# One gathered row at a time, paired score blocks and a partly rounded value product in a Hymba/PEER encoder layer

## The chip, the cores and the metric

One core of one Trainium2 chip runs the whole layer as one program. The metric is the device time of one execution, in microseconds (us).

## The reference

Two sequences of 256 tokens, each with 16 meta tokens ahead, go through one encoder layer of width 1024: norm, one input projection, a short gated convolution beside attention, an output projection, and then a retrieval mixer (PEER). The mixer is what the change is about. Each token scores 16 sets of 128 keys, picks 16 experts of 16384 for each of 8 heads, and mixes them:

```python
def chunk(args):
    xc, ic, gc = args
    uc = jnp.take(u_tab, ic, axis=0)
    a = jax.nn.gelu(jnp.einsum('thkd,td->thk', uc, xc), approximate=False) * gc
    vc = jnp.take(v_tab, ic, axis=0)
    return jnp.einsum('thk,thkd->td', a, vc)
```

So a token takes 128 rows of `u_tab` (a dot with its x, then gelu, then the gate) and the 128 rows of `v_tab` with the same numbers (a weighted sum). All inputs are float32.

## The kernel before, in words

The kernel does the mixer in two ways at once. The **second sequence** is done densely: all 16384 experts are multiplied with its 256 tokens. The **first sequence** is done sparsely: 2 tiles of 128 tokens times 128 picks are 256 gathered rows, one row a partition, each DMA bringing u and v beside each other (8 KB a partition, 1.0486 MB in all). The stages, in order:

1. `front(0, ...)` and `projections`: the first sequence's layer and its keys, with weights split in two rounded parts (`whi`, `wlo`) and three products for one; it gives the picks of tile 0.
2. `front(1, ...)` and `projections` for the second sequence (190 to 401 us in the profile). Beside it run tile 1's picks and the first gathered rows.
3. The scores (401 to 907 us): 128 blocks of 128 experts. A 512 KB load of `u` on SP's queue, 8 matmuls into one PSUM bank `pSj`, gelu on ACT, into the big tile `A` (`Al`, `Ah`). The task `gates_dense` runs beside it: it builds the dense gates by one-hot products on TensorE (`oi`, `gh`, `gl` into `pgm`), four tokens at a time, and multiplies them into `A`.
4. The values (907 us to the end): 128 blocks, each a 512 KB load of `v` and four 512-column matmuls in full float32, A(j) times v, that accumulate in four PSUM banks `acc`.

Rows are gathered through stages 2 to 4. `bg(us)` is called after each piece of TensorE work with an estimate of its length; a share of it (`SF` in the front, `SR`, `SS`, `SMAX` later) is credited, and each 2.65 us of credit calls `gather()`. In stage 4 the calls are spread evenly over the blocks, by `left`. One call of `gather()` takes, for a ring of four row buffers: the gelu and gate of the row whose dot is done (`g_weight`, two one-column ops on ACT), the dot of the oldest row that is on its way (`g_dot`, on DVE), the value sum of the row before (`g_val`, on DVE, into `h`), and then the DMA of a new row into the freed buffer (`g_issue`, on POOL's queue, tied by `sync_dep` to the latest matmul). When tile 0's last row is summed, `h` is stored and the next `h` is loaded into the same buffer, and so is the next `x`.

A scheduler places the instructions of each engine; the code fixes only what it names in a dependency. DVE, ACT and POOL each work strictly in their order, so whatever stands behind a waiting instruction waits too.

Names: `grow` is a gathered row, `dots` its dots, `xg` and `hg` the tile's x and h (after the change both `xh`), `w` a weight slab, `tau` how many tokens' gates are done, `r_done` how many score blocks are in `A`. In the profile, L63 is the line of the helper through which DVE and ACT instructions are recorded.

## Time and profile before

| | |
|---|---|
| median of 3 runs | 1365.17 us (1362.3 to 1374.88) |
| the profiled execution's own time | 1362.99 us |
| its span | 1360.9 us |
| busy: TensorE, DVE, ACT, POOL | 1298.1, 1031.9, 437.4, 414.0 us |
| DMA moved | 460.19 MB, mean 338 GB/s |
| busy time of the 256 dots and 256 value sums on DVE | 312.5 and 327.9 us |
| DVE idle ahead of dots, ended by a row's DMA | 138.6 us |
| DVE idle ahead of value sums, ended by ACT | 67.9 us |

The span is what the profile covers; the execution took 2.1 us more. Busy times of different engines overlap. A wait is the idle time of an engine before an instruction, put down to what ended it; idle time of an engine on which nobody waits costs nothing.

### The profile page before, as it was taken

How to read it: one execution, taken by the hardware profiler on the slowest of the kernel's cores; microseconds unless marked ns; L12 is line 12 of the kernel's file. 1: busy time of each engine (PE TensorE's matmuls, PEld its weight loads, DVE VectorE, ACT ScalarE, POOL GpSimd, SP SyncE). 2: the span in 40 equal slices, each digit the busy share in tenths (PEclk: the TensorE clock that was granted, in tenths of full speed). 3: DMA queues.
4: the chain of work that ended last, by engine and by line, in shares of the span. 5: the costliest groups of instructions: out<-in, count | busy, mean ns of one | idle time of the engine just before them, and what ended most of it. 6: DMA issues, size and time to landing. Idle time of an engine off the chain costs nothing. (4 is left out here: it accounts for less than half of the span.)

```text
span 1360.9 us, 17663 instructions
## 1 busy us (share of the span) xinstructions
PE 1298.1 (95%) x5870; PEld 927.9 (68%) x5870; DVE 1031.9 (76%) x2356; ACT 437.4 (32%) x1467; POOL 414.0 (30%) x480
## 2 busy tenths in 40 slices
PE   5999998998999887999999999999999999999998
PEld 5888986677888666888888888774443344444443
DVE  5656999776999889988888996676666665666665
ACT  4555533732221312555555543111111111111111
POOL 2111224331344342222221221223455523433331
PEclk9999999999999998999999999999999999999999
DMA  6434637577998999999999999999999999999997
GB/s 218 126 109 153 206 107 263 199 272 301 366 341 332 390 399 374 348 368 367 355 368 359 366 375 376 377 416 416 417 417 417 418 416 417 416 417 416 416 417 294
DMA packets 90234, 460.19 MB, mean 338 GB/s; under 512 B 10512, under 2 KB 11024, under 8 KB 57120
## 3 DMA queue, kind: packets, MB, share of 16 engines
q0 software_dynamic: 37296, 270.02, 49.7%
q1 hardware_dynamic: 50832, 182.33, 36.1%
q10 hardware_dynamic: 2016, 6.72, 1.3%
q8 instruction: 46, 0.75, 0.2%
q14 instruction: 44, 0.36, 0.1%
HBM read 454.81 MB, written 4.19 MB: 337 GB/s over the span
## 5 line engine op out<-in xcount | busy, mean ns | idle before, releaser
L157 POOL DMA_INDIRECT grow<-in_uv,eidx x256 | 331.9, 1297 | 694.8 <-PE acc L947 118.1
L130 PE MATMUL pSj<-xr,u 128*128 128x256 f32 x2048 | 465.6, 385 | 12.6 <-ACT Al L63 10.5
L130 PEld LDWEIGHTS pSj<-xr,u 128*128 128x128 f32 x2048 | 386.3, 192 | 68.7 <-ACT Al L63 14.5
L63 DVE SCALAR_TENSOR_TENSOR grow<-grow,xg 128x1024 f32<-128x1024 f32 x256 | 312.5, 1221 | 143.6 <-DMA grow<-in_uv,eidx 138.6
L63 DVE SCALAR_TENSOR_TENSOR hg<-grow,dots,hg 128x1024 f32<-128x1024 f32 x256 | 327.9, 1281 | 77.4 <-ACT dots L63 67.9
L947 PE MATMUL acc<-v,Al 128*128 128x512 f32 x752 | 329.9, 596 | 1.8
L947 PEld LDWEIGHTS acc<-v,Al 128*128 128x128 f32 x752 | 140.6, 190 | 190.6 <-issue 164.2
L63 ACT ACTIVATE dots<-dots 128x1 f32<-128x1 f32 x256 | 51.6, 202 | 552.2 <-DVE grow L63 551.2
L947 PE MATMUL acc<-v,Ah 128*128 128x512 f32 x272 | 118.0, 594 | 0.2
L947 PEld LDWEIGHTS acc<-v,Ah 128*128 128x128 f32 x272 | 51.3, 190 | 66.7 <-issue 62.1
L63 ACT ACTIVATE gl<-oj,glo 128x128 f16<-128x128 f16 x256 | 88.8, 393 | 10.9 <-DVE oj L63 5.1
L63 ACT ACTIVATE dots<-dots,gate_all 128x1 f32<-128x1 f32 x256 | 75.1, 294 | 7.5 <-ACT dots L63 0.6
L63 DVE TENSOR_TENSOR wlo<-w,whi 128x1024 fp32r<-128x1024 f32 x42 | 51.0, 1217 | 19.9 <-ACT whi L63 13.9
L63 ACT ACTIVATE pSj<-pSj 128x256 f32<-128x256 f32 (+39 forms) x94 | 26.6, 284 | 110.7 <-PE pSj L130 110.7
L130 PE MATMUL pqq<-xr,w 128*128 128x256 f32 x256 | 59.5, 385 | 0.7 <-DMA w<-in_wq 0.7
L130 PEld LDWEIGHTS pqq<-xr,w 128*128 128x128 f32 x256 | 48.2, 194 | 7.3 <-DMA w<-in_wq 1.1
L63 ACT ACTIVATE whi<-w 128x1024 fp32r<-128x1024 f32 x42 | 43.9, 1055 | 20.5 <-PE pqq L130 9.5
L130 PE MATMUL pc<-xT,w 128*128 128x258 f32 (+1 forms) x192 | 47.5, 390 | 1.1 <-DVE rb L63 0.6
L130 PEld LDWEIGHTS pc<-xT,w 128*128 128x128 f32 x192 | 34.9, 192 | 8.6 <-issue 2.5
L130 PE MATMUL pqq<-xr,whi 128*128 128x256 f32 x128 | 37.2, 292 | 0.0
L130 PE MATMUL pqq<-xrl,whi 128*128 128x256 f32 x128 | 36.4, 285 | 0.3 <-DVE xrl L63 0.3
L894 PE MATMUL pgm<-gh,oi 128*128 128x128 f16 x256 | 35.5, 219 | 1.3 <-DVE gh L63 1.3
(268 smaller groups left out, 1539.3 us busy)
## 6 DMA issues: line engine op xcount, KB each, us to landing
u<-in_u_t SPq DMA_DIRECT2D x128, 512.0 KB, 6.8
v<-in_v_n SPq DMA_DIRECT2D x128, 512.0 KB, 14.9
w<-in_w_in SPq DMA_DIRECT2D x36, 512.0 KB, 4.3
w<-in_wq SPq DMA_DIRECT2D x32, 512.0 KB, 5.0
w<-in_w_out SPq DMA_DIRECT2D x16, 512.0 KB, 4.8
grow<-in_uv,eidx POOLq DMA_INDIRECT x256, 9.2
hdram<-h ACTq DMA_DIRECT2D x3, 512.0 KB, 3.0
h<-in_xp SPq DMA_DIRECT2D x2, 512.0 KB, 7.3
```

Source lines behind the costliest of these rows:

```text
L63: i = f(*a, **k)
L130: i = pe.matmul(out, st_(c, a), mv(c, b), start=(n == 0), stop=(n == NC * len(terms) - 1))
L157: i = pool.indirect_dma_start(out=r, out_offset=None, in_=uv, in_offset=bass.IndirectOffsetOnAxis(ap=eidx[:, t, k:k + 1], axis=0))
L894: pe.matmul(pg[:, r, :], oi[:, k, :], gh[:, k, :], start=True, stop=False)
L947: i = pe.matmul(acc[t][q], A(j)[:, t * P:(t + 1) * P], vb[:, q * 512:(q + 1) * 512], start=j == 0, stop=j == P - 1, skip_group_check=True)
```

## The change

- **Ring.** The four ring buffers become pools of one buffer each, `ga1` to `ga4`, and a fifth, `ga0`, holds x and h of tile 0 side by side. When the first row of tile 1 is issued, the next ring buffer takes tile 1's x and h (both loads are issued there), and `ga0` joins the ring in its place.
- **Order of a call.** `gather()` first does the value sum of the row whose weight is ready, then issues the next row into that buffer, then the dot of the oldest row, and its gelu and gate at once.
- **Credit.** `SF` is 0.6 for 0.5. Adding the credits up, 27 rows are issued in the second sequence's front where it was 22. The later stages issue as many as before, and 101 rows are left for the values where it was 106.
- **Scores.** Two blocks share one bank-wide tile (four of them, as there were four tiles before), and `experts` empties them together, one pair later. The gate task waits 4.0 us of credit more, casts the identity on ACT, and its products run one step behind the building of their operands.
- **Values.** `v` is loaded by pairs of blocks, 1 MB, rows of 8 KB, into three buffers; `wp` is closed first. Of four blocks the last (`j % SPL == SPL - 1`) is split: ACT rounds A(j) and v, DVE takes the rests, and three rounded products take the place of the full one. `hd_` is loaded at the end on SP's queue.

```diff
-SF = 0.5
+SF = 0.6
+SPL = 4
...
-    ga = ctx.enter_context(sb("ga", GBUF, "right"))
+    ga = [ctx.enter_context(sb(f"ga{i}", 1, "right")) for i in range(GBUF + 1)]
+    wpx = ExitStack()
+    wp = wpx.enter_context(sb("wp", 4, "right"))
...
     def g_issue():
...
+        if t == 1 and k == 0:
+            ring_free.append(ring.pop(0))
+            gctx["next"] = row_pair()
+            pool.dma_start(gctx["next"][0], xdram)
+            pool.dma_start(gctx["next"][1], hdram[0])
+            ring.append(ga[0])
...
     def g_val():
...
         if t == 0 and k == P - 1:
             pool.dma_start(yp[0:P, :], gctx["h"])
-            h = gc.tile([P, D], F32, tag="hg", name="hg1")
-            pool.dma_start(h, hdram[0])
-            gctx["h"] = h
+            gctx["h"] = gctx["next"][1]
...
     def gather(n=1):
         for _ in range(n):
-            if len(pend) + len(vals) >= len(ring) or not queue:
-                if vals:
-                    g_weight()
-                if pend:
-                    g_dot()
-                while len(vals) > 1:
-                    g_val()
...
-            while queue and len(pend) + len(vals) < len(ring):
+            if vals:
+                g_val()
+            while queue and len(pend) < len(ring):
                 g_issue()
+            if pend and (len(pend) >= len(ring) or not queue):
+                g_dot()
+                g_weight()
...
+        yield 4.0
...
-        dve.tensor_copy(ident16, ident)
+        act.activation(ident16, ident, AF.Copy)
...
+                steps.append((t * P + s0, oi, gh, gl))
+                if len(steps) > 1:
+                    gate_products(*steps.pop(0))
...
+    def experts(j, p):
+        part, o = (Al, j) if j < JH else (Ah, j - JH)
+        a = part[:, o:o + 2]
+        n = tau[0]
+        if n:
+            act.activation(p[:, :, :n], p[:, :, :n], AF.Gelu)
+        if n < 256:
+            act.activation(a[:, :, n:], p[:, :, n:], AF.Gelu)
+        if n:
+            dve.tensor_tensor(a[:, :, :n], p[:, :, :n], a[:, :, :n], op=ALU.mult)
...
-        p = psS.tile([P, 256], F32, tag="S", name="pSj")
+        if j % 2 == 0:
+            p = psS.tile([P, 2, 256], F32, tag="S", name="pSj")
...
+    wpx.close()
-    vp = ctx.enter_context(sb("vp", 2, "right"))
+    vp = ctx.enter_context(sb("vp", 3, "right"))
...
+    def values(j):
+        if j % 2 == 0:
+            vpair[0] = vp.tile([P, 2, D], F32, tag="v", name="v")
+            nc.sync.dma_start(vpair[0], vn3[:, j:j + 2])
+        vb = vpair[0][:, j % 2]
+        if j % SPL != SPL - 1:
+            return ((A(j), vb),)
...
+        act.activation(ah, A(j), AF.Copy)
+        act.activation(vh, vb, AF.Copy)
+        dve.tensor_tensor(al, A(j), ah.bitcast(F32), op=ALU.subtract)
+        dve.tensor_tensor(vl, vb, vh.bitcast(F32), op=ALU.subtract)
+        return ((ah, vh), (al, vh), (ah, vl))
...
+    hd_ = vp.tile([P, 2, D], F32, tag="v", name="hd")
+    nc.sync.dma_start(hd_, hdram[1:3].rearrange("t p d -> p t d"))
```

Line numbers differ between the two programs by up to 56. Three places show how the order moves. The first is SP's queue at the end of the scores; `u` are score loads, `v` value loads. Before:

```order
L918 DMA u<-in_u_t 128x1024 x115
L941 DMA v<-in_v_n 128x1024 x2
L918 DMA u<-in_u_t 128x1024 x13
L941 DMA v<-in_v_n 128x1024 x126
L956 DMA out_yp<-hg_7901 128x1024
```

After the change:

```order
L953 DMA u<-in_u_t 128x1024 x128
L981 DMA v<-in_v_n 128x2048 x64
L1009 DMA hd<-hdram 128x2x1024
L1012 DMA out_yp<-xh 128x1024
L1017 DMA out_ys<-hd 128x512 x2
```

Two value loads that stood ahead of the last 13 score loads are gone from there, a load is twice as large, and the load of `hd` stands behind the values.

The second is DVE in the middle of the scores, where gates (`oi`, `gh`, `pgm`), score blocks (`pSj`) and gathered rows alternate. Before:

```order
L63 TENSOR_TENSOR oi<-dup,io 128x512
L63 SCALAR_TENSOR_TENSOR Al<-pgm,Al 128x65x4
L63 SCALAR_TENSOR_TENSOR grow,dots<-grow,xg_1560 128x1024
L63 SCALAR_TENSOR_TENSOR hg_1564<-grow,dots,hg_1564 128x1024
L63 TENSOR_TENSOR Al<-pSj,Al 128x116
L63 TENSOR_TENSOR gh<-oj,dup 128x512
```

After the change:

```order
L64 TENSOR_TENSOR Al<-pSj,Al 128x2x116
L64 SCALAR_TENSOR_TENSOR Al<-pgm,Al 128x66x4
L64 SCALAR_TENSOR_TENSOR xh<-grow,dots,xh 128x1024
L64 SCALAR_TENSOR_TENSOR grow,dots<-grow,xh 128x1024
L64 TENSOR_TENSOR oi<-dup,io 128x512
L64 TENSOR_TENSOR gh<-oj,dup 128x512
```

The value sum stands ahead of the dot instead of behind it, and a score block comes in pairs.

The third is DVE in the middle of the values, with the buffers' numbers, so that a row can be followed. Before:

```order
L63 SCALAR_TENSOR_TENSOR grow_8879,dots_84<-grow_8879,xg1_7854 128x1024
L63 SCALAR_TENSOR_TENSOR hg1_7901<-grow_8879,dots_84,hg1_7901 128x1024
L63 SCALAR_TENSOR_TENSOR grow_8891,dots_84<-grow_8891,xg1_7854 128x1024
L63 SCALAR_TENSOR_TENSOR hg1_7901<-grow_8891,dots_84,hg1_7901 128x1024
L63 SCALAR_TENSOR_TENSOR grow_8903,dots_84<-grow_8903,xg1_7854 128x1024
```

After the change:

```order
L64 SCALAR_TENSOR_TENSOR grow_8615,dots_96<-grow_8615,xh_7377 128x1024
L64 TENSOR_TENSOR vhl_8167<-v_8660,vhl_8167 128x1024
L64 TENSOR_TENSOR al_8673<-Al_3648,ah_8672 128x256
L64 SCALAR_TENSOR_TENSOR xh_7377<-grow_8615,dots_96,xh_7377 128x1024
L64 SCALAR_TENSOR_TENSOR grow_8645,dots_96<-grow_8645,xh_7377 128x1024
L64 SCALAR_TENSOR_TENSOR xh_7377<-grow_8645,dots_96,xh_7377 128x1024
L64 SCALAR_TENSOR_TENSOR grow_8655,dots_96<-grow_8655,xh_7377 128x1024
L64 SCALAR_TENSOR_TENSOR xh_7377<-grow_8655,dots_96,xh_7377 128x1024
L64 SCALAR_TENSOR_TENSOR grow_8667,dots_96<-grow_8667,xh_7377 128x1024
L64 TENSOR_TENSOR vhl_8167<-v_8712,vhl_8167 128x1024
```

A row's dot and value sum stand together in both; new are the two subtractions of a split block, once in three or four rows, with a value sum behind them.

## Rows read from the trace of the kernel before

**Rows 1.** The span by stage: from and to, length, busy us (and instructions) of each engine, TensorE's granted clock, DMA's busy share, GB/s.

```profile
core 0: us, PE busy (x) PEld busy (x) DVE busy (x) ACT busy (x) POOL busy (x), PEclk, DMA share, GB/s
0.00:190.00 190.00, 172.28 (x1330) 159.39 (x1331) 133.52 (x418) 97.92 (x203) 31.51 (x85) 1.00 0.50 159
190.00:331.00 141.00, 127.95 (x626) 101.30 (x625) 117.44 (x398) 58.54 (x154) 50.31 (x98) 0.99 0.65 235
331.00:401.00 70.00, 65.75 (x326) 57.20 (x325) 62.45 (x271) 19.02 (x68) 29.16 (x49) 0.98 0.93 346
401.00:550.00 149.00, 130.33 (x584) 110.56 (x583) 134.69 (x346) 37.67 (x132) 52.55 (x58) 0.95 0.96 374
550.00:850.00 300.00, 298.72 (x1738) 260.65 (x1738) 256.73 (x523) 156.41 (x641) 67.47 (x67) 1.00 0.95 365
850.00:907.00 57.00, 55.02 (x251) 46.84 (x250) 37.97 (x56) 11.13 (x44) 14.28 (x13) 1.00 0.98 393
907.00:1329.00 422.00, 419.99 (x963) 179.92 (x961) 271.19 (x325) 53.75 (x216) 165.01 (x107) 1.00 1.02 417
1329.00:1361.00 32.00, 28.04 (x65) 12.08 (x64) 17.91 (x23) 2.98 (x12) 3.75 (x4) 0.98 0.71 286
```

**Rows 2.** The line of the page with what DMA moved, GB/s in 40 equal slices of the span.

```profile
GB/s 218 126 109 153 206 107 263 199 272 301 366 341 332 390 399 374 348 368 367 355 368 359 366 375 376 377 416 416 417 417 417 418 416 417 416 417 416 416 417 294
```

**Rows 3.** Pieces of the chain that ended last, in the values: start, us, what.

```profile
907.50 103.01 PE acc L947 x240
...
1010.53 18.50 DMA v<-in_v_n
...
1100.83 106.89 PE acc L947 x248
```

**Rows 4.** DMA from 907 us to the end: packets and MB, and the value loads.

```profile
DMA packets 34973, 184.97 MB, mean 407 GB/s; under 512 B 3890, under 2 KB 3890, under 8 KB 20662
...
v<-in_v_n SPq DMA_DIRECT2D x123, 512.0 KB, 15.1
```

**Rows 5.** What TensorE's matmuls waited for, 401 to 907 us: us in total, times, the longest.

```profile
PE pSj L130 <- ACT Al L63: 10.5, 6, 4.2
PE pi L864 <- DVE ident L63: 8.0, 1, 8.0
PE pSj L130 <- DVE Ah L63: 2.0, 4, 0.9
PE pgm L894 <- DVE gh L63: 1.3, 1, 1.3
```

**Rows 6.** DVE in the middle of the values: a row's dot, its value sum, the next dot.

```profile
1121.32 1.22 DVE L63 SCALAR_TENSOR_TENSOR grow<-grow,xg 128x1024 f32<-128x1024 f32 x1 [0.78 <-DMA grow<-in_uv,eidx]
...
1123.15 1.28 DVE L63 SCALAR_TENSOR_TENSOR hg<-grow,dots,hg 128x1024 f32<-128x1024 f32 x1 [0.60 <-ACT dots L63]
1125.11 1.23 DVE L63 SCALAR_TENSOR_TENSOR grow<-grow,xg 128x1024 f32<-128x1024 f32 x1 [0.67 <-DMA grow<-in_uv,eidx]
```

**Rows 7.** What DVE waited for, 190 to 401 us: us in total, times, the longest.

```profile
DVE hg L63 <- ACT dots L63: 3.6, 3, 1.8
```

**Rows 8.** Groups of instructions over the whole span: shape, count, busy us, mean ns of one, idle us before them.

```profile
L63 DVE TENSOR_TENSOR wlo<-w,whi 128x1024 fp32r<-128x1024 f32 x42 | 51.0, 1217 | 19.9 <-ACT whi L63 13.9 <-PE pc L130 5.6
...
L63 ACT ACTIVATE whi<-w 128x1024 fp32r<-128x1024 f32 x42 | 43.9, 1055 | 20.5 <-PE pqq L130 9.5 <-PE pc L130 3.2 <-PE po L130 3.0
...
L63 ACT ACT_TABLE_LOAD x18 | 23.1, 1283 | 2.0 <-PEq L1017 1.7
...
L63 DVE TENSOR_TENSOR Ah<-pSj,Ah 128x256 f32<-128x256 f32 x17 | 7.0, 416 | 0.0
```

**Rows 9.** TensorE in the first sequence's output projection, the first and the last of 15 rounded products that follow each other: start, us, instruction.

```profile
106.08 0.28 PE L130 MATMUL po<-whi,catT 128*128 128x256 f32 x1
...
107.73 0.28 PE L130 MATMUL po<-whi,lo 128*128 128x256 f32 x1
```

**Rows 10.** POOL in order of time around the change from tile 0 to tile 1: start, us, instruction, in brackets the idle time before it and what ended it.

```profile
837.39 0.57 POOL L166 DMA_DIRECT2D out_yp<-hg  x1 [1.91 <-DVE hg L63]
838.27 0.98 POOL L157 DMA_INDIRECT grow<-in_uv,eidx  x1 [0.30 <-issue]
848.60 0.57 POOL L168 DMA_DIRECT2D hg<-hdram  x1 [9.35 <-DMA out_yp<-hg]
857.66 1.80 POOL L157 DMA_INDIRECT grow<-in_uv,eidx  x1 [8.50 <-DVE Ah L63]
```

**Rows 11.** The store of h at the change of tiles, from the page's list of DMA issues: count, size, us to landing.

```profile
out_yp<-hg POOLq DMA_DIRECT2D x1, 512.0 KB, 10.9
```

**Rows 12.** DMA from 1010 to 1101 us: packets, MB and share of each queue (q0 is POOL's, q1 SP's), then loads with their count, size and median us to landing.

```profile
q0 software_dynamic: 3427, 24.92, 66.0%
q1 hardware_dynamic: 3553, 12.95, 35.5%
...
v<-in_v_n SPq DMA_DIRECT2D x25, 512.0 KB, 18.9
grow<-in_uv,eidx POOLq DMA_INDIRECT x23, 11.2
```

**Rows 13.** What DVE waited for, 907 to 1357 us: us in total, times, the longest.

```profile
DVE grow L63 <- DMA grow<-in_uv,eidx: 95.3, 112, 2.8
DVE hg L63 <- ACT dots L63: 63.9, 107, 0.6
```

More of the change, by code (lines that the diff above doesn't have):

```diff
@@ L148, in encoder_layer, with row_pair @@
     gctx = {}
-    ring = [ga] * GBUF
+    ring = ga[1:]
+    def row_pair():
+        p = ring_free.pop(0).tile([P, 2 * D], F32, tag="g", name="xh")
+        return p[:, :D], p[:, D:]
+    ring_free = [ga[0]]
     def g_issue():
@@ L160, in g_issue, with order @@
         pend.append((t, k, r))
+    def order(i, before):
+        tc.add_manual_dep(i.ins, before.ins.name,
+                          mybir.DependencyInfo(mybir.DependencyClass.NoSync, mybir.DependencyReason.DATA),
+                          reason="order")
     def g_val():
         t, k, r = vals.pop(0)
-        dve.scalar_tensor_tensor(gctx["h"], r[:, D:], dots[:, k:k + 1], gctx["h"], op0=ALU.mult, op1=ALU.add)
+        before = last[0]
+        i = dve.scalar_tensor_tensor(gctx["h"], r[:, D:], dots[:, k:k + 1], gctx["h"], op0=ALU.mult, op1=ALU.add)
+        order(i, before)
         if t == 0 and k == P - 1:
             pool.dma_start(yp[0:P, :], gctx["h"])
-            h = gc.tile([P, D], F32, tag="hg", name="hg1")
-            pool.dma_start(h, hdram[0])
-            gctx["h"] = h
+            gctx["h"] = gctx["next"][1]
     def g_weight():
@@ L174, in g_weight @@
         i = act.activation(dots[:, k:k + 1], dots[:, k:k + 1], AF.Gelu)
-        tc.add_manual_dep(i.ins, before.ins.name,
-                          mybir.DependencyInfo(mybir.DependencyClass.NoSync, mybir.DependencyReason.DATA),
-                          reason="order")
+        order(i, before)
         act.activation(dots[:, k:k + 1], dots[:, k:k + 1], AF.Copy, scale=gate_all[:, t, k:k + 1])
@@ L184, in g_dot @@
                                      accum_out=dots[:, k:k + 1])
-        tc.add_manual_dep(i.ins, before.ins.name,
-                          mybir.DependencyInfo(mybir.DependencyClass.NoSync, mybir.DependencyReason.DATA),
-                          reason="order")
+        order(i, before)
         if t == 0 and k == P - 1:
-            x = gc.tile([P, D], F32, tag="xg", name="xg1")
-            pool.dma_start(x, xdram)
-            gctx["x"] = x
+            gctx["x"] = gctx["next"][0]
         vals.append((t, k, r))
@@ L858, in gates_dense, with gate_products @@
         ident16 = og.tile([P, P], F16, name="ident16")
-        dve.tensor_copy(ident16, ident)
+        act.activation(ident16, ident, AF.Copy)
         iv = io.rearrange("p (a r) -> p a r", r=2)
         v4 = lambda x: x.rearrange("p t (a r) -> p t a r", r=2)
+        steps = []
+        def gate_products(a, oi, gh, gl):
+            pg = psg.tile([P, OC, P], F32, tag="g", name="pgm")
+            for r in range(OC):
+                pe.matmul(pg[:, r, :], oi[:, r, :], gh[:, r, :], start=True, stop=False)
+                pe.matmul(pg[:, r, :], oi[:, r, :], gl[:, r, :], start=False, stop=True)
+            n = r_done[0]
+            pj = pg.rearrange("p t j -> p j t")
+            parts = [(part, lo, hi, min(max(n, lo), hi)) for part, lo, hi in ((Al, 0, JH), (Ah, JH, P))]
+            for part, lo, hi, m in parts:
+                if m < hi:
+                    act.activation(part[:, m - lo:hi - lo, a:a + OC], pj[:, m:hi], AF.Copy, scale=1.0 / GSH)
+            for part, lo, hi, m in parts:
+                if m > lo:
+                    av = part[:, 0:m - lo, a:a + OC]
+                    dve.scalar_tensor_tensor(av, pj[:, lo:m], 1.0 / GSH, av, op0=ALU.mult, op1=ALU.mult)
+            tau[0] = a + OC
         for t in range(2):
@@ L911, in encoder_layer @@
     share.update(a=SS, b=SBS)
-    ut = {}
+    late = []
+    def experts(j, p):
[8 more added lines that the diff above has]
+            dve.tensor_tensor(a[:, :, :n], p[:, :, :n], a[:, :, :n], op=ALU.mult)
+        r_done[0] = j + 2
     for j in range(P):
```

72 lines of the change are left out of this document (28 added, 44 removed).

## The prediction

> **What bounds the kernel now.** I read the table by stage first [rows 1]. From 401 to 1357 us TensorE is busy nearly all the time, at a granted clock of 1.00 (the 2.4 GHz level) but for the first part; before 331 us the change touches little. Two stages hold 956 us: the scores, 401 to 907 (506.3 us), and the values, 907 to the end (453.9 us). In the table and the GB/s line [rows 1, 2] the reader is to see that the two are unlike. In the scores DMA moves 365 to 393 GB/s and its rate wavers; in the values it stands at 417 for 422 us on end. So the values have two limits side by side. TensorE: 240 records, which are 30 blocks, took 103.01 us, 3.434 us a block [rows 3]. DMA: 184.97 MB left after 907 us [rows 4], at 417 GB/s 443.6 us, and 10.3 us more for the thinner end. The chain [rows 3] goes through value products, and in between through an 18.5 us load of v. The chain names who came last, not who is full; the flat 417 says that DMA is full.
>
> In the scores TensorE waits for 21.8 us in all, in four places [rows 5]: 10.5 for ACT to empty score banks, 8.0 for the cast of the identity on DVE, 2.0 and 1.3 for DVE. The rest of the 506.3 us is its own work.
>
> **The front, 331 us.** SF 0.6 for 0.5 issues 27 rows instead of 22 during the second sequence's front: five more rows at a dot and a value sum of 1.22 and 1.28 us [rows 6], 12.5 us of DVE. DVE idles 23.6 us between 190 and 331 (141.0 less 117.4 busy), TensorE 13.1. Hidden wholly it costs 0, wholly on the path 12.5; below nothing it can reach -3.6, the waits of value sums for ACT that go in this stretch and the next [rows 7]. I take +4, a third of the top, since DVE's idle time covers the work but not at the right moments. The order of ACT has two more table loads than before, 1.28 us each [rows 8]; ACT is busy 58.5 of these 141 us, and they cost nothing unless a bank waits. The rounded weights of the first sequence keep four buffers, so the first 190 us stay.
>
> **The scores.** Pairs take the place of single blocks, in four banks as before, so eight blocks may wait instead of four; the cast moves to ACT and the gate task starts 4.0 us of credit later. The 10.5 and the 8.0 us [rows 5] should go: 3.4 us a block times four further blocks is more than the longest wait, 4.2 us. What is late next is DVE, whose 2.0 and 1.3 us I leave. Ends: -21.8, and 0 if the same time comes back as waits on DVE, which is busy 134.7 of the first 149 us. I take -18.5. Gelu and multiply on pairs save a start each on ACT and DVE, which TensorE hides; I count nothing.
>
> **The values: TensorE.** Of every four blocks one goes as three rounded products. A rounded product of 256 columns goes out every 0.118 us (14 starts in 1.65 us [rows 9]); 512 columns are not in the trace. Twice that is 0.236 us, twelve of them 2.83 us; if a 512-column product costs half of one full-precision record (3.434 / 8 = 0.429), 2.58. The nearer row is the first: 2.83. So 96 x 3.434 + 32 x 2.83 = 420.2 us, and with 3.8 us behind it 424 against 453.9.
>
> **The values: DMA.** The bytes don't follow. Left to issue are 101 rows instead of 106: -5.24 MB at 1.0486 MB a row. At the change of tiles, the second thing that goes: POOL issues no row from 838.27 to 857.66 [rows 10], as it waits for h to be stored, then loads the next h, and DVE waits for that load. With the next x and h loaded ahead (the same two transfers, on the same queue, four rows earlier) only the store is waited for (10.9 us to land [rows 11]), since ga0 joins the ring behind it: 19.4 - 10.9 = 8.5 us, two rows at today's 4.2 us each (450 us for 106 rows), -2.1 MB. One value block less is there at the start: +0.5. That leaves 178.1 MB, 427.2 us at 417 GB/s, with the thin end 10.3: 437.5. The first loads: the order of SP puts the first pair behind the last score block and each pair behind a whole buffer, so I add 2 us. The load of hd moves from ACT's queue in mid-stage to the end of SP's: the same 1 MB, asked for four blocks before the last product, some 13 us; it costs nothing if it lands like the store of half its size, in 10.9 us [rows 11], and a few us if not. 439.5 us: -14.4, and not the -30 of TensorE. The split's worth is mostly hidden behind the transfers.
>
> What the trace shows of how the two streams share: between 1010 and 1101 us the gathers' queue moved 3427 packets and the value queue 3553, nearly as many, but 24.92 MB against 12.95, as a gathered row is 8 KB and a value row 4 KB [rows 12]. That starved the values (18.9 us to land, with TensorE waiting). The change loads two adjacent rows as one of 8 KB: if it stays one packet, v may have half of the bandwidth and is never short; the sum above rests on the total alone. The Trainium skill, page "DMA: Bandwidth & Descriptors", section "Queues, rings and completion order", says that an engine takes its rings in turn, a packet at a time; the equal counts agree. The same page calls 4 KB the preferred size of a packet; the mean gather packet of 7.3 KB here does not keep to it. Its section "Where 436 GB/s comes from" gives a ceiling of 435 GB/s: by that, an estimate, the value stage would be 420 us; the 417 that every slice shows is what I use.
>
> **The values: DVE and ACT.** This is where the change adds waits. The split of one block costs ACT 1.06 us and a shorter op for A, DVE 1.22 and 0.42 [rows 8]. The order shows that DVE has dot and value sum of one row next to each other in this stage, before and after: the 0.60 us wait for gelu [rows 6, 13] stays, though the diff says at once. A row takes DVE 3.12 us (1121.32 to 1125.11 less 0.67), so four blocks with 3.25 rows need 10.1 + 1.64 = 11.8 of 13.1 us. Behind the subtraction, which waits for vhl to be read out and for its pair to land, stand the next value sum and dots; POOL's next gather waits for those. Its cover is 1.3 us in four blocks. Ends: 0, and 3.0 us per four blocks (95.3 us of waits on rows [rows 13] over 32 groups) if today's waits are simply added. I take 0, since those waits are what DMA's pace causes and shrink as DVE fills.
>
> **Sum.** 1360.9 + 4 - 18.5 - 14.4 = 1332.0 us of span; the profiled run took 1362.99, 2.1 more: 1334 us. The profiled run is 0.2% under the median of 1365.17, so I compare with the median: -2.3%.
>
> **Rivals.** A: DMA gives way. With 8 KB rows on both queues the rate rises above 417 and TensorE bounds the values: 424 us, 1360.9 + 4 - 18.5 - 29.9 + 2.1 = 1319. For it: no row shows 8 KB packets on both queues, so 417 is the rate of another mixture. Against it: in 422 us it never moved.
>
> B: the values gain nothing. Groups of four blocks take 14.05 us as today (449.6 / 32), because DVE and DMA trade waits: 1360.9 + 4 - 18.5 + 2.1 = 1348.5. For it: 11.8 us of DVE against 13.1 is thin. Against it: fewer bytes at a full queue.
>
> C, slower: DVE stands in line behind the split. It waits for ACT's copy of v (1.06 us), which waits for its pair; with three buffers the pair is asked for two blocks before ACT comes to it. If the wait for rows stays 3.0 us as well, a group takes 11.8 + 3.0 + 1.06 = 15.9 us, the values 32 x 15.9 + 3.8 = 512.6, the total 1360.9 + 4 - 18.5 + 58.7 + 2.1 = 1407. It decides from 14.6 us a group: there the total is the median of today, at 15.0 it is 1% over. For it: a load of v half as large lands in 15.1 us [rows 4]. Against it: those loads queue behind five of their own, the pairs behind one or two.
>
> **How the numbers follow.** A measurement of this kernel tells about 1% from no change: 1351.5 and 1378.8 are the bounds. Forecast 0.50, A 0.20, B 0.20, C 0.10. Faster takes the forecast nearly whole, A whole and a third of B: 0.76; same, the rest of B and a little of the forecast: 0.14; slower 0.10. Range: from the lower end of A (1319 less 3.3 of score waits and the -3.6 + -4 of the front: 1308) to past B with its front at the top (1348.5 + 8.5, and part of the score gain lost: 1366); left out are C and a little below.
>
> **What would show it.** Right: the scores some 488 us with TensorE's waits under 5; DMA at 417 through the values; value groups at 13.1 to 13.5 us; some 7 MB less to move after the last score; no long gap of POOL at the change of tiles but for the store. Wrong: a rate well above 417 (A), waits of value products for vhl or al, or DVE idle on v (B, C), a front much over 335 us, or scores that still take 500.

## The result and the profile after

The changed kernel takes 1360.4 us (median of 15 runs, 1356.9 to 1363.6), the kernel before 1367.3 in as many runs beside it: a ratio of 0.9946, 95% interval 0.9929 to 0.9964. It is faster, by 0.5% and not by the 2.3% forecast; by the prediction's own bounds (1% either way) this is no change, to which it had given 0.14. The profiled execution has a span of 1359.7 us, 1.2 less than before (1360.9), and its stages are these (columns as in [rows 1]):

```profile
0.00:190.00 190.00, 171.35 (x1322) 158.66 (x1322) 132.34 (x410) 97.69 (x202) 30.68 (x85) 1.00 0.49 159
190.00:345.60 155.60, 135.67 (x634) 105.67 (x635) 132.00 (x423) 64.63 (x171) 63.38 (x104) 0.95 0.69 245
345.60:427.40 81.80, 69.41 (x328) 60.52 (x327) 68.34 (x310) 19.13 (x65) 25.40 (x50) 0.92 0.88 322
427.40:930.00 502.60, 484.64 (x2567) 416.06 (x2566) 426.72 (x849) 193.68 (x720) 163.05 (x139) 0.99 0.97 375
930.00:1357.00 427.00, 421.03 (x1152) 216.75 (x1152) 309.55 (x385) 92.75 (x274) 119.73 (x102) 1.00 1.00 414
```

Against [rows 1], with each stage cut at its first product:

| stage | before | after | forecast of the difference | measured |
|---|---|---|---|---|
| second sequence's front | 141.2 | 155.6 | +4 | +14.4 |
| second q-projection | 70.0 | 81.8 | 0 | +11.8 |
| scores | 506.1 | 502.6 | -18.5 | -3.5 |
| values to the end | 453.6 | 429.7 | -14.4 | -23.9 |
| sum | | | -28.9 | -1.2 |

The signs of three terms held and none of the sizes; the large terms missed in both directions. What TensorE waited for, first from 190 to 427 us (five of the six longest; not shown is `v_sb` with 3.4 us, which took 3.2 before), then in the scores, where [rows 5] stood:

```profile
PE pn L366 <- ACT qs L64: 6.2, 1, 6.2
PE pcr L668 <- POOL cstat L662: 4.7, 2, 4.1
PE pn L366 <- DMA Ah<-in_skT: 4.0, 1, 4.0
...
PE pc L137 <- ACT cs L64: 3.3, 1, 3.3
PE pqq L137 <- DMA w<-in_wq: 2.0, 1, 2.0
...
PE pgm L882 <- DVE gh L64: 10.4, 1, 10.4
PE pgm L882 <- DVE oi L64: 3.2, 1, 3.2
PE pSj L137 <- DMA u<-in_u_t: 2.2, 5, 1.5
```

The 10.5 us for ACT and the 8.0 for the identity are gone, as forecast. In their place stand 13.6 us for the one-hots gh and oi of the first gate product, one wait in one place. TensorE's idle time in the scores falls only from 21.9 to 18.0 us. DVE just ahead of that place (start, us, instruction, in brackets idle time and releaser):

```profile
544.45 0.22 DVE L64 TENSOR_TENSOR idx_j<-Ah 128x128 f16<-128x128 f16 x1
...
550.08 1.22 DVE L64 SCALAR_TENSOR_TENSOR grow<-grow,xh 128x1024 f32<-128x1024 f32 x1 [0.64 <-DMA grow<-in_uv,eidx]
...
551.91 1.28 DVE L64 SCALAR_TENSOR_TENSOR xh<-grow,dots,xh 128x1024 f32<-128x1024 f32 x1 [0.60 <-ACT dots L64]
553.86 1.23 DVE L64 SCALAR_TENSOR_TENSOR grow<-grow,xh 128x1024 f32<-128x1024 f32 x1 [0.67 <-DMA grow<-in_uv,eidx]
...
571.71 0.29 DVE L64 SCALAR_TENSOR_TENSOR glo<-pg,g 128x128 f32<-128x128 f32 x1 [1.55 <-ACT g L64]
```

TensorE in the same stretch, the last of its transposes for the gates and the first gate product:

```profile
557.79 0.28 PE L901 MATMUL pg<-ident,gate_all 128*128 128x128 f32 x1
...
575.73 0.27 PE L882 MATMUL pgm<-gh,oi 128*128 128x128 f16 x1 [10.36 <-DVE gh L64]
```

Between the last index (544.45) and the first op of the gates (571.71) stand rows alone, one every 3.8 us, each waiting for its transfer. TensorE had finished the transposes for the gates by 558.1 us. DVE is not full here; it stands behind rows that come as fast as DMA brings them, and ACT behind their gelus. The stage up to the last index in two stretches (columns as in [rows 1]) shows where DVE fell behind:

```profile
427.40:476.00 48.60, 48.60 (x216) 42.37 (x216) 46.95 (x180) 14.03 (x33) 18.58 (x31) 0.95 0.88 327
476.00:544.50 68.50, 65.96 (x291) 53.71 (x290) 59.69 (x90) 13.14 (x45) 29.07 (x18) 1.00 1.02 416
```

In the first 48.6 us DVE is full, busy for 46.95, mostly with the selection of keys, and DMA moves 327 GB/s. After that DVE has idle time, but the rows come only as DMA, now at 416 GB/s, brings them.

In the projection the clock is part of the loss. TensorE there, the same products soon after a wait and later:

```profile
364.39 1.19 PE L366 MATMUL pn<-Ah,qs 128*128 128x128 f32 x4 [4.04 <-DMA Ah<-in_skT]
...
367.93 4.93 PE L137 MATMUL pqq<-xr,w 128*128 128x256 f32 x16
...
373.15 3.62 PE L137 MATMUL pqq<-xr,w 128*128 128x256 f32 x16
```

Sixteen products take 4.93 us soon after the idle 4.04 us and 3.62 later; the granted clock is 0.74 from 360 to 373 us and 1.00 from 373 to 400. Over the front and the projection TensorE's busy time rises from 128.2 + 65.7 to 135.7 + 69.4 us at granted clocks of 0.95 and 0.92 instead of 0.99 and 0.98: 11.2 of the 26.2 us lost there. The Trainium skill, page "TensorE: Matmul & The Clock Gate", section "Part 1: The HAM clock gate (the "warmup" mystery)", says that the clock gate has two levels only. By that the 0.92 of the stage is a mean over stretches at either level, and the two durations fit that.

The values, for one group of four blocks on TensorE:

```profile
1111.73 1.48 PE L1001 MATMUL acc<-vhl,ah 128*128 128x512 f32 x4
1113.05 1.09 PE L1001 MATMUL acc<-vhl,al 128*128 128x512 f32 x4
1113.98 1.09 PE L1001 MATMUL acc<-vhl,ah 128*128 128x512 f32 x4
1114.91 10.46 PE L1001 MATMUL acc<-v,Al 128*128 128x512 f32 x24
1124.81 1.48 PE L1001 MATMUL acc<-vhl,ah 128*128 128x512 f32 x4
```

A group starts 13.1 us after the one before (1111.73 to 1124.81), as forecast (13.1 to 13.5). A rounded 512-column product goes out every 0.93 / 4 = 0.232 us, where I took 0.236. Three full blocks at 3.434 us and twelve such products are 13.09 us, so this group runs at TensorE's own pace; 19 of the 31 distances between groups in the stage are no longer than 13.08 us. DMA from 930 us to the end, as [rows 4], and from 1010 to 1101, as [rows 12]:

```profile
DMA packets 24978, 177.29 MB, mean 412 GB/s; under 512 B 2771, under 2 KB 2771, under 8 KB 3667
...
hd<-hdram SPq DMA_DIRECT2D x1, 1024.0 KB, 12.1
...
DMA packets 5264, 38.32 MB, mean 421 GB/s; under 512 B 588, under 2 KB 588, under 8 KB 588
...
q1 hardware_dynamic: 1968, 14.30, 37.7%
...
v<-in_v_n SPq DMA_DIRECT2D x14, 1024.0 KB, 9.6
```

177.3 MB were to move (forecast 178.1), at 421 GB/s in that window (forecast 417); a v pair lands in 9.6 us where half of it took 18.9. At the change of tiles POOL's longest time without a row is 10.0 us instead of 19.4 [rows 10], close to the 10.9 forecast:

```profile
848.10 0.94 POOL L178 DMA_INDIRECT grow<-in_uv,eidx  x1 [0.30 <-issue]
858.12 1.19 POOL L178 DMA_INDIRECT grow<-in_uv,eidx  x1 [9.09 <-DVE xh L64]
```

But this wait ends with a value sum and not with the store. The store, issued at 833.34 us, landed 11.7 us later, and the first row behind it was issued at 845.28.

### The profile page after: what moved, and what is told of

Same layout as the page of the kernel before. It is cut to its first block, busy times and chain, and to the rows that moved or that the text cites. A ratio compares the mean times of both kernels' runs of the same rounds, so it can differ in the third digit from the quotient of the medians.

```text
span 1359.7 us, 17703 instructions
## 1 busy us (share of the span) xinstructions
PE 1282.1 (94%) x5998; PEld 957.7 (70%) x5998; DVE 1069.0 (79%) x2373; ACT 467.9 (34%) x1431; POOL 402.2 (30%) x480
## 4 chain that ended last, share of the span: by engine, by line
PE 39%; DMA 20%; DVE 4%; issue 3%; ACT 0%; DVEq 0%; POOL 0%; SPq 0%; POOLq 0%
PE pSj L137 21%; DMA grow<-in_uv,eidx 19%; PE acc L1001 16%; DVE xh L64 1%; DMA v<-in_v_n 1%; PE pgm L882 1%; PE pgm L883 1%; DVE grow L64 1%; DVE vhl L64 1%; DVE Ah L64 1%; ACT dots L64 0%; DVE Al L64 0%; DVE al L64 0%; DVE hd L64 0%; DVE oi L64 0%
## 5 line engine op out<-in xcount | busy, mean ns | idle before, releaser
L64 DVE SCALAR_TENSOR_TENSOR grow<-grow,xh 128x1024 f32<-128x1024 f32 x256 | 312.4, 1220 | 96.8 <-DMA grow<-in_uv,eidx 96.6
L64 DVE SCALAR_TENSOR_TENSOR xh<-grow,dots,xh 128x1024 f32<-128x1024 f32 x256 | 327.4, 1279 | 57.2 <-ACT dots L64 56.8
L1001 PE MATMUL acc<-v,Al 128*128 128x512 f32 x568 | 247.8, 592 | 1.3 <-DMA v<-in_v_n 1.3
L1001 PEld LDWEIGHTS acc<-v,Al 128*128 128x128 f32 x568 | 107.8, 190 | 128.0 <-issue 124.4
L1001 PE MATMUL acc<-v,Ah 128*128 128x512 f32 x200 | 87.3, 592 | 0.0
L1001 PE MATMUL acc<-vhl,ah 128*128 128x512 f32 x256 | 81.8, 441 | 0.0
L64 ACT ACTIVATE gl<-oj,glo 128x128 f16<-128x128 f16 x256 | 81.6, 398 | 0.1
L1001 PEld LDWEIGHTS acc<-v,Ah 128*128 128x128 f32 x200 | 38.0, 190 | 44.7 <-issue 44.0
L1001 PEld LDWEIGHTS acc<-vhl,ah 128*128 128x128 f32 x256 | 48.1, 188 | 23.3 <-issue 14.1
L137 PE MATMUL pc<-xT,w 128*128 128x258 f32 (+1 forms) x192 | 48.6, 398 | 4.0 <-ACT cs L64 3.3
L882 PE MATMUL pgm<-gh,oi 128*128 128x128 f16 x256 | 36.1, 220 | 13.5 <-DVE gh L64 10.4
L64 DVE TENSOR_TENSOR gh<-oj,dup 128x512 f16<-128x512 f16 x64 | 27.0, 422 | 25.2 <-PE pgm L882 24.0
```

Of the source, the lines that this page charges most:

```text
L64: i = f(*a, **k)
L137: i = pe.matmul(out, st_(c, a), mv(c, b), start=(n == 0), stop=(n == NC * len(terms) - 1))
L882: pe.matmul(pg[:, r, :], oi[:, r, :], gh[:, r, :], start=True, stop=False)
L1001: i = pe.matmul(acc[t][q], a[:, t * P:(t + 1) * P], v[:, q * 512:(q + 1) * 512], start=j == 0 and n == 0, stop=j == P - 1 and n == len(ter ...
```

## The experiments

Stage times of one profiled execution each, in us; ratio to the kernel before with its 95% interval. Seven of these kernels have the changed kernel's front (the changed one, 4, 6, 11, 12, 13, 15): their fronts read 152.8 to 157.4, so a stage is known to some 2 us either way.

| run | front | proj. | scores | values | median | ratio |
|---|---|---|---|---|---|---|
| changed | 155.6 | 81.8 | 502.6 | 429.7 | 1360.4 | 0.995 (0.993 to 0.996) |
| 1 old order of a row | 154.9 | 80.0 | 516.2 | 475.5 | 1420.9 | 1.040 (1.034 to 1.045) |
| 2 SF 0.5 | 138.7 | 80.8 | 504.2 | 440.4 | 1356.7 | 0.992 (0.990 to 0.995) |
| 3 gelu a call later | 150.6 | 75.6 | 507.2 | 430.4 | 1352.7 | 0.990 (0.986 to 0.993) |
| 4 no split | 153.7 | 82.8 | 503.8 | 443.7 | 1374.5 | 1.005 (1.003 to 1.008) |
| 5 before + new order | 137.5 | 78.6 | 498.5 | 449.2 | 1357.4 | 0.994 (0.992 to 0.997) |
| 6 gates later | 154.9 | 80.2 | 499.6 | 431.6 | 1358.3 | 0.994 (0.992 to 0.996) |
| 7 combined | 141.5 | 71.7 | 499.5 | 431.3 | 1334.3 | 0.977 (0.974 to 0.980) |
| 8 three in flight | 149.7 | 79.4 | 501.5 | 429.3 | 1351.5 | 0.989 (0.987 to 0.992) |
| 9 combined, other share | 142.9 | 73.5 | 485.8 | 437.3 | 1332.0 | 0.976 (0.970 to 0.983) |
| 10 deferral in proj. only | 138.6 | 80.9 | 491.6 | 431.3 | 1336.4 | 0.980 (0.976 to 0.984) |
| 11 v in 4 KB rows | 153.3 | 83.8 | 499.4 | 436.9 | 1365.6 | 0.999 (0.997 to 1.001) |
| 12 single blocks | 157.4 | 83.0 | 494.7 | 434.6 | 1358.6 | 0.996 (0.994 to 0.998) |
| 13 shifted rows | 155.7 | 77.1 | 504.1 | 432.2 | 1361.4 | 0.995 (0.992 to 0.997) |
| 14 all together | 140.2 | 77.3 | 492.0 | 434.2 | 1333.8 | 0.973 (0.970 to 0.977) |
| 15 share alone | 152.8 | 83.6 | 484.5 | 434.8 | 1349.1 | 0.986 (0.983 to 0.990) |

**1. The old order of a row.** In gather(), at each call:

```diff
-            if vals:
-                g_val()
-            while queue and len(pend) < len(ring):
-                g_issue()
-            if pend and (len(pend) >= len(ring) or not queue):
-                g_dot()
-                g_weight()
+            if len(pend) + len(vals) >= len(ring) or not queue:
+                if vals:
+                    g_weight()
+                if pend:
+                    g_dot()
+                while len(vals) > 1:
+                    g_val()
...
+            while queue and len(pend) + len(vals) < len(ring):
+                g_issue()
```

> The changed kernel with the order of a row as it was before the change: at each call the gelu of the row whose dot was queued one call ago, then the next dot, then the value sum, then the next gather. All else of the change stays (SF 0.6, pairs, split, loads ahead). Theory L (ACT stands in line: a gelu queued right behind its dot blocks ACT until that dot, and so until its gathered row, has come, and all ACT work behind it is late): the second sequence's front returns from 155.5 to about 145 us, the second q-projection from 81.9 to about 71, the wait of 10.4 us for gh at the start of the gate products goes; the values keep about 430; time about 1360 - 10.5 - 11 - 10 = 1328 us. Rival R (the five further rows of SF 0.6 and their traffic fill the front, whatever the order of a row): front and projection stay within 4 us of 155.5 and 81.9, time 1356 to 1364. Rival M (the new order is what made the values 24 us faster): front and scores gain as in L, but the values go back to about 445 to 454: 1345 to 1352.

Theory L fell: front and projection stay (154.9, 80.0). Rival M was right that the values grow, and by far too small: they take 475.5 us.

```profile
941.12:1416.60 475.48, 436.89 (x1152) 217.76 (x1152) 309.86 (x392) 94.15 (x279) 127.34 (x105) 0.98 0.96 378
```

DMA falls to 378 GB/s; DVE waits 160.5 us for rows in this stage, where it waited 68.0 in the changed kernel. In this order the next gather waits for a value sum that stands behind the next dot, and so behind the next row's landing: POOL waits 175.0 us for value sums in this stage (66.3 in the changed kernel), and TensorE 29.5 us for the split's operands.

This order is not the one that the kernel before executes in the values. There a value sum follows the dot of its own row and waits 0.60 us for the gelu between them [rows 6, 13]. The change also ties each value sum to the DVE instruction written just ahead of it (`order(i, before)` in `g_val()`, a line that the diff above does not print), and run 1 keeps that tie. So here a value sum follows the dot of the next row, and in the whole stage DVE never waits for ACT. DVE in run 1:

```profile
1121.56 1.23 DVE L64 SCALAR_TENSOR_TENSOR grow<-grow,xh 128x1024 f32<-128x1024 f32 x1 [1.07 <-DMA grow<-in_uv,eidx]
...
1122.71 1.28 DVE L64 SCALAR_TENSOR_TENSOR xh<-grow,dots,xh 128x1024 f32<-128x1024 f32 x1
1128.23 1.23 DVE L64 SCALAR_TENSOR_TENSOR grow<-grow,xh 128x1024 f32<-128x1024 f32 x1 [4.24 <-DMA grow<-in_uv,eidx]
```

The 46 us are the price of this order with the split. What the split would cost in the order that the kernel before really has in the values, no run shows, and so it is not shown that the split needs the new order.

**2. SF alone.** `SF = 0.5` for 0.6.

> The changed kernel with SF 0.5 as before the change (22 instead of 27 rows issued in the second sequence's front), the new order of a row kept. Theory L: the front stays long, since each row still blocks ACT; a fifth fewer rows give back about a fifth of the 14.4 us, 3 us, and the later rows cost the values about 12 us of DMA (five rows of 1.05 MB at 420 GB/s): 1360 - 3 + 12 = 1369, or 1360 if the projection gives some back as well. Rival R: the front returns to about 142 to 145 us and the projection to 70 to 72, and the scores or values take the five rows: 1340 to 1348.

```profile
190.00:328.71 138.71, 126.83 (x634) 101.42 (x635) 122.40 (x410) 51.48 (x153) 56.69 (x100) 0.99 0.71 253
...
913.74:1354.10 440.36, 422.52 (x1152) 216.39 (x1152) 319.03 (x396) 95.10 (x282) 131.34 (x106) 1.00 0.99 412
```

The front is back at 138.7, further than R had it (142 to 145); R was wrong on the projection, which stays at 80.8, and on the whole, 1356.7. The five rows cost 16.9 us in the front: 8.0 of idle TensorE (19.9 against 11.9) and 8.9 of busy time, at a granted clock of 0.95 instead of 0.99. They return 10.7 us in the values.

**3. The gelu a call later.** g_weight() moved from behind g_dot() to the front of the next g_val().

> The changed kernel with the gelu alone moved: it is queued at the next call, right ahead of its value sum, instead of right behind its dot; DVE and POOL keep the new order (value sum, next gather, next dot). Theory L: ACT is no longer blocked by a dot, so front, projection and the gh wait go back as in the first of these runs, at the price of a wait of DVE for ACT before each value sum (0.6 us or more, 256 rows, hidden where DVE has room): 1330 to 1345. Rival P (it is POOL, whose next gather waits for the value sum, with the statistics' power operations in line behind it): front 151 to 158 us and projection 78 to 84 us as in the changed kernel, 1355 to 1365 or more.

1352.7 us lies between the two theories, and the reason that L gave does not hold. In the trace ACT still waits for dots (26.7 us in the projection, 6.3 at most; 33.7 in the changed kernel), and the wait for gh grows to 17.6 us. Front and projection are 5 and 6 us shorter; the projection's long wait for the query evacuation fell to 1.7 us.

**4. No split.** `SPL = 256`.

> The changed kernel without the split: all 128 value blocks go as full-precision products; pairs of v as 8 KB rows, loads ahead and the rest stay. By the prediction's step that DMA bounds the values and the split is mostly hidden: values within 10 us of 429.7 (TensorE would need 128 x 3.434 = 439.6 us, DMA about 425), so 1362 to 1372. Rival T (TensorE bounds the values, the split is what gave the gain): 128 x 3.434 + 4 = 444 or more, 1374 to 1384, with DMA below 410 GB/s in the values.

443.7 us in the values, TensorE busy in 439.7 of them and DMA at 399 GB/s: rival T. The split is worth 14.0 us in this stage, and my step that it is mostly hidden behind DMA is wrong.

**5. The new order alone, in the kernel before.** The gather() of the changed kernel in the other; nothing else.

> The kernel before with the new order of a row alone (value sum, next gather, next dot, gelu at once); SF 0.5, single blocks, no split, 4 KB rows of v. Theory D (the order costs the second q-projection and gives to the values, the front's loss is SF's): front of the second sequence 138 to 144 us, projection 76 to 82 (70.0 before), scores 500 to 512, values 440 to 447 (TensorE's own 128 x 3.434 = 439.6, since a gather no longer stands behind a dot that waits for a row): 1355 to 1368. Rival O (the order costs the front too): front 146 to 152, 1365 to 1376. Rival N (the values' 10 us that the changed kernel without the split had gained come from the 8 KB rows and the loads ahead, not from the order): values 452 to 455, 1368 to 1378.

```profile
327.51:406.10 78.59, 68.26 (x327) 59.00 (x325) 66.20 (x303) 18.94 (x66) 36.96 (x50) 0.93 0.86 318
406.10:904.59 498.49, 485.53 (x2566) 419.07 (x2566) 429.37 (x896) 213.83 (x815) 161.98 (x138) 0.99 0.97 375
904.59:1353.80 449.21, 444.27 (x1025) 192.96 (x1024) 282.35 (x340) 55.76 (x224) 142.25 (x108) 1.00 1.00 407
```

D on front and projection: the order alone makes the projection 8.6 us longer and its clock 0.93. It gives 4.4 us to the values, between D and N, and 7.6 to the scores, more than D had allowed for. With single blocks and the old gate code this kernel is as fast as the whole change.

**6. The gates later.** `yield 9.0` for 4.0 ahead of them.

> The changed kernel with the credit that the gate task waits for raised from 4.0 to 9.0: its first products stand some three score blocks (10 us) later in TensorE's program. Theory G (TensorE meets the gates before DVE and ACT, which run some 14 us behind it, have made the one-hots; the wait only changed its name): the waits for gh and oi, 13.6 us, fall under 5, scores 490 to 495, 1349 to 1352. Rival H (whatever stands ahead, the score stage is bound by DVE's and DMA's work until the gates are done, and the wait comes back elsewhere): scores 500 or more, 1358 to 1362.

H: gh and oi still cost 11.4 us. The first gate product starts at 585.4 us, 9.7 later than in the changed kernel, and waits only 2.2 us less: DVE's one-hots moved by nearly as much as TensorE's work. No run sets the 4.0 back to nothing.

**7. Combined.** SF 0.5, the gelu a call later until the scores, and

```diff
-SS = 0.64
+SS = 0.71
+SE = 0.56
-    share.update(a=SS, b=SBS)
+    share.update(a=SE, b=SBS)
+        share["a"] = SS          (where the gates start)
```

> The changed kernel with what the runs so far point to: SF 0.5; the gelu queued at the next call until the scores begin, at once from there on; gathers at a share of 0.56 until the gates start and 0.71 after (0.64 throughout in the changed kernel). 102 rows are left for the values, as in the changed kernel (101). If the parts add up: front 155.6 - 17, projection 81.7 - 6, scores 502.7 - 8 (less DVE work ahead of the gates), values 429.7 + 2: 1360 - 29 = 1331. Rival: the rows that leave the front are paid for in the scores, where DVE is busy 43 of 50 us: scores 510 or more, 1345 to 1350.

1334.3 us for 1331: the sum nearly came out, but partly by luck. The front is 2.9 us longer than added up, the projection 4.0 shorter and the scores 4.8 longer.

**8. Three gathers in flight** until the scores: `len(ring) - 1` in both conditions of gather().

> The changed kernel with three gathers in flight instead of four until the scores begin; order of a row as changed. Theory Q (the fourth gather in flight makes loads of weights and subkeys land late, 9.8 us for the subkeys against 4.9 before): waits of TensorE for wq and skT, 6.0 us in the projection, fall under 2, projection 74 to 77 us, front 152 to 156: 1353 to 1356. Rival (those loads are late because they are asked for late or because more rows are gathered per us): projection 80 to 83, 1358 to 1363.

Faster (1351.5), yet against theory Q: TensorE still waits 5.9 us for wq and skT and the projection stays at 79.4. The gain is in the front, 149.7; what in it is shorter I did not isolate.

**9. Fewer rows ahead of the gates.** Run 7 with `SE = 0.4`, `SS = 0.76`.

> The combined kernel (SF 0.5, gelu at the next call until the scores) with the share of gathers at 0.40 ahead of the gates and 0.76 after, instead of 0.56 and 0.71: some seven rows leave the stretch ahead of the gates, 103 are left for the values (102). Theory S (at 0.64 a score block asks for 0.845 rows of 1.05 MB and 0.52 MB of u in 3.4 us, 415 GB/s, all that DMA gives, so DVE and ACT, which stand behind rows, never catch up with TensorE before the gates): at 0.40 the demand is 317 GB/s, the waits for gh and oi (13.6 us in the changed kernel, 10.1 in the combined one) fall under 3, scores 490 to 495, 1325 to 1331. Rival H (the lag is the top-k chain's own, rows or not): waits of 8 or more remain, 1333 to 1340.

The scores fall to 485.8 us. The waits are 6.9 in all, not under 3, but the longest is 2.9. The values give 6 us of it back, with one row more to move.

**10. The deferral in the projection only.** Run 7 with the gelu at once in the front.

> The combined kernel with the gelu deferred in the second q-projection alone (at once in the front and from the scores on). If the deferral is what shortened the projection and costs the front a little, front 137 to 139.5 (141.5), projection 71 to 73 (71.7): 1330 to 1333. Rival (the projection was shorter because the front left other rows and another clock behind it): projection 76 to 81, 1335 to 1341.

The front as expected (138.6), the projection not (80.9, with 6.7 us of wait for the query evacuation again). The deferral in that stage is not what shortened it. The scores take 7.9 us less than in run 7, with 3.9 us of waits for one-hots instead of 10.1, though the code is the same from the scores on: most of what the projection lost came back there. A gain in one stage is not yet one of the whole.

**11. v in rows of 4 KB.**

```diff
-            nc.sync.dma_start(vpair[0], vn3[:, j:j + 2])
+            for r in range(2):
+                nc.sync.dma_start(vpair[0][:, r], vn3[:, j + r])
```

> The changed kernel with each pair of value rows loaded as two transfers with rows of 4 KB instead of one with rows of 8 KB; buffers and order the same. Theory E (packets of 8 KB give the value queue its share and lift DMA from 417 to 421 GB/s): DMA 410 to 417 GB/s in the values, products wait for v, values 436 to 446: 1366 to 1376. Rival (the rate is what it is at a full queue, packets or not): values 428 to 433, 1358 to 1363.

Values 436.9, DMA from 1010 to 1101 us:

```profile
DMA packets 7071, 37.38 MB, mean 411 GB/s; under 512 B 790, under 2 KB 790, under 8 KB 4232
...
q1 hardware_dynamic: 3880, 14.10, 38.9%
```

Theory E on the stage: with 8 KB rows it is 421 GB/s in this window, and the stage is 7.2 us shorter. The window flatters the rows of 8 KB: with 4 KB it holds a dip to 362 GB/s (1074 to 1080 us). In most slices of the whole stage the rates are 414 to 419 with 4 KB, as in the kernel before, and 420 to 424 with 8 KB. No wait of TensorE for v is seen; v is late for the split, where DVE waits 53.6 us for ACT's copy of v (1.5 in the changed kernel). The Trainium skill, page "DMA: Bandwidth & Descriptors", section "SWDGE vs HWDGE vs iDMA", puts a packet at 4096 bytes or less by preference; in this pair of runs the larger rows are the faster ones, and the measurement decides here.

**12. Single score blocks.** Four banks of one block, experts() after each product.

> The changed kernel with the score blocks evacuated one by one as before the change, four banks of one block each; all else stays. The prediction's step (pairs take away the waits of TensorE for empty banks): 10 us or more come back as waits for ACT or DVE, scores 512 to 520, 1369 to 1378. Theory S (the wait is for DVE and ACT being behind ahead of the gates; pairs only let TensorE run further ahead before it waits): the waits move to the score banks but sum to the same 13 to 18 us, scores 499 to 507, 1357 to 1364.

The pairs are not what helps: without them the scores are 494.7 us, 7.9 less, with 6.4 us of waits for ACT and 2.3 for the one-hots. The values take 4.9 more, and the whole is the same within its interval. Neither theory held: one had expected scores of 512 or more, the other 499 to 507 with waits of 13 to 18 us in all, and the waits are 9.0.

**13. Rows of the projection shifted.** `credit["a"] -= 1.8` at its start. In the changed kernel ACT shows this at the stage's end:

```profile
425.49 0.20 ACT L64 ACTIVATE dots<-dots 128x1 f32<-128x1 f32 x1 [6.35 <-DVE grow L64]
425.72 0.29 ACT L64 ACTIVATE dots<-dots,gate_all 128x1 f32<-128x1 f32 x1
425.93 0.36 ACT L64 ACTIVATE qs<-pqq 128x256 f32<-128x256 f32 x1
```

The last qs stands behind a gelu whose dot stands on DVE behind a head's top-k.

> The changed kernel with 1.8 us less credit for gathers at the start of the second q-projection: the rows of the stage come a little later, as many before the scores as in the changed kernel, and no gelu stands directly ahead of the last query evacuation on ACT any more. Theory L2 (one gelu ahead of the last evacuation, which waits for a dot behind a head's top-k, holds TensorE 6.2 us): that wait falls under 2, projection 74 to 77 us, 1352 to 1356. Rival (the evacuation is late because DVE's top-k is, whatever stands on ACT; or another wait takes its place): projection 79 to 83, 1357 to 1362.

```profile
PE pn L366 <- ACT qs L64: 2.4, 1, 2.4
...
PE pgm L883 <- DVE gh L64: 15.4, 1, 15.4
PE pgm L883 <- DVE oi L64: 1.9, 1, 1.9
```

Nearly L2 on the stage (77.1 us, the wait 2.4), the rival on the whole: 1361.4. The stage is 4.7 us shorter, and the waits at the gates grow by 3.7, to 17.3 us. TensorE came to them some 9 us sooner, the one-hots only 4.

**15. The share of rows alone**, at the changed kernel: `SE = 0.46` ahead of the gates, `SS = 0.71` after.

> The changed kernel with the share of gathers 0.46 ahead of the gates and 0.71 after instead of 0.64 throughout; as many rows in all. Theory S (at 0.64 the rows ahead of the gates ask for all that DMA gives, DVE and ACT stay behind TensorE, and after the gates DMA has room that nobody uses): waits for gh and oi 13.6 us to under 4, scores and values together from 932 to 918 to 924, 1346 to 1352. Rival (the gain of the combined kernels came from SF, the deferral and the projection): 1357 to 1362.

```profile
426.40:910.92 484.52, 480.34 (x2568) 415.15 (x2566) 422.05 (x844) 191.70 (x715) 154.41 (x138) 1.00 0.98 385
910.92:1345.70 434.78, 423.11 (x1152) 217.93 (x1152) 313.27 (x390) 94.90 (x279) 119.55 (x103) 0.99 0.99 412
```

TensorE's waits for the one-hots, and then DVE's first op for the gates, which started at 571.71 in the changed kernel:

```profile
PE pgm L884 <- DVE gh L65: 1.4, 1, 1.4
PE pgm L884 <- DVE oi L65: 0.7, 1, 0.7
```

```profile
552.48 0.29 DVE L65 SCALAR_TENSOR_TENSOR glo<-pg,g 128x128 f32<-128x128 f32 x1 [12.20 <-ACT g L65]
```

Theory S. The waits are 2.1 us, and the roles are reversed: DVE is early and waits 12.2 us. The scores are 18.1 us shorter, scores and values together 13.0. DMA moves 385 GB/s in the scores instead of 375.

**14. All together**: SF 0.5, the shift of run 13, `SE = 0.46`, `SS = 0.75`, gelu at once.

> The changed kernel with SF 0.5, the shift of the credit at the projection, and the share of gathers 0.46 ahead of the gates and 0.75 after; gelu at once throughout. If the parts add up: front 138.7, projection 75, scores 489, values 433, 1328. Rival (from the scores on DMA is full, so only bytes count and not where TensorE waits): scores and values together 923 or more as in the kernel with the deferral in the projection alone, projection 80: 1335.

1333.8 us, 2.7% under the kernel before, nearer to the rival (1335) than to the sum (1328): scores and values take 926.2 us together, the projection 77.3. Runs 7, 9, 10 and 14 cannot be told apart.

## Why the prediction was wrong

**The front, +4 taken, +14.4 measured.** The step that failed is the upper end, "wholly on the path 12.5", of which I took a third: I priced five rows in DVE time alone. Run 2 shows 16.9, and 8.9 of it is busy time of TensorE at a lower granted clock. The waits that grew most are for POOL's cstat and ACT's cs, both behind rows on their engines: with SF 0.5 they wait 1.0 and 0.5 us instead of 4.7 and 3.3. What lowered the clock stays open: runs 7 and 9 have 11.2 us of idle TensorE in the front, less than run 2 with 11.9, at 0.96 and 0.95 instead of 0.99.

**The projection, left out of the sum, +11.8.** I read what the change does on DVE's side and gave this stage no term, although it moves every gather, dot and gelu in it. Run 5 shows that the order alone makes 8.6 of it. The rows of the two profiles give 8.1 us more idle TensorE (waits of 12.2 against 4.1) and 3.6 of busy time at a granted clock of 0.92 instead of 0.98. Run 13 removes most of the largest wait and gains nothing on the whole, as DVE is still late at the gates. The waits for wq and skT remain in all versions with the new order (3.5 to 7.6 us); what makes these loads late stays open, as run 8 speaks against the depth of the ring.

**The scores, -18.5 taken, -3.5 measured.** The named waits went, and came back elsewhere, which the text had as its other end ("0 if the same time comes back as waits on DVE"). The failed step is "3.4 us a block times four further blocks is more than the longest wait": a buffer covers a consumer that is late once, not one that stays late. At a share of 0.64 a block of 3.4 us asks for 3.5 x 0.64 / 2.65 = 0.845 rows of 1.05 MB and 0.52 MB of u, 415 GB/s, and from 476 us on DMA moves 416. So the lag that DVE had by then it could not make up ahead of the gates. Run 15 shows the remedy and its size: 18 us of scores, 13 of the sum. It takes rows from DVE and from DMA at once; that DMA sets the pace is read from DVE's waits for each row, and no run separates the two. And the pairs, to which I gave most of the gain, are not needed for it: run 12 without them has shorter scores.

**The values, -14.4 taken, -23.9 measured.** The step that failed is "the flat 417 says that DMA is full", from which I let the bytes alone set the stage: "The split's worth is mostly hidden behind the transfers." Without the split the stage takes 443.7 us with DMA at 399 GB/s, and TensorE is busy for 439.7 of them (run 4): TensorE is the limit there, and the split is worth 14.0 of the 23.9. Everything else gives 9.9. The rows had said so: 240 products in 103.01 us [rows 3] are 3.434 us a block, TensorE's own pace, with DMA at 417 beside it. After the change most groups run at that pace, which is the limit of rival A, whose 424 us are nearer to the measured 429.7 than my 439.5. DMA is close behind: 177.3 MB at 421 GB/s are 421.1 us, beside 421.0 of busy TensorE, and five rows more cost 10.7 us (run 2). The rate rose by 1%, to 421 from 417; run 11 shows that the 8 KB rows do it. DVE did not become the limit: its split op causes 2.9 us of TensorE's waits.

**Dot and gelu at once.** "the 0.60 us wait for gelu [rows 6, 13] stays" was right for most rows (45.2 us, 78 times in the values, instead of 63.9 and 107). But I drew from it that the order of a row does nothing there, and run 5 shows 4.4 us for it. Run 1 shows rival C's mechanism, DVE in line behind the split, at 46 us, in an order that neither kernel has in the values.

So the sum missed by 27.7 us: 10.4 in the front, 11.8 in the projection, 15.0 in the scores, and 9.5 gained back in the values. These 9.5 are luck, as the DMA sum behind the -14.4 took the wrong limit. Two of the signs of being wrong that the prediction named came: a front much over 335 us (345.6) and scores that still take 500 (502.6).

## What to carry to other kernels

When a wait is to be buffered away, ask whether its releaser is late once or behind on average; if it is behind, most of the wait only changes its name, and the work ahead of it has to move. A stage in which a change moves instructions needs its own term, even where its table looks balanced, and a term for idle TensorE needs the granted clock beside it. A full DMA does not show that DMA is the limit: look whether the other engine also runs at its own pace. Where two limits lie within a few per cent, test each alone: here the useful parts (the split, the 8 KB rows) were outweighed by two numbers that set how many rows run where. And when an old order is put back for a test, compare the order that was executed, not the lines of the program.

## What was not expected of the hardware

TensorE's own work in the front took 135.7 us at a granted clock of 0.95 and 126.8 at 0.99 (run 2), with eight us more or less of idle time between it: here the lower clock cost as much as the waits. The idle time alone does not set it, as runs 7 and 9 show. And rows of 8 KB on both queues moved 420 to 424 GB/s in most slices of the values, where 8 KB beside 4 KB moved 414 to 419 (run 11).
